# Weight differences issued later, the value product as three matmuls, and block products in runs: one change to a float32 encoder kernel

## The chip, the cores and the metric

The kernel runs on one core of a Trainium2 chip. The metric is the device time of one execution in microseconds (us). Three runs of the kernel before gave 2529.61, 2530.25 and 2532.10 us, so the median is 2530.25 us. A separate execution was profiled, and everything below that speaks of rows, waits or starts is from that one.

## The reference

The reference is a two-layer encoder over 272 tokens (16 meta tokens and 256 others) of width 2048. Each layer has a mixing part (an input projection, attention, a Fourier branch, gates and an output projection) and a feed-forward part. The change touches the feed-forward part alone:

```python
h2 = _rmsnorm(h_stream, norm_ffn[i])
up = h2 @ w_up[i]
u_gate = _dwconv3_centred(up[..., :D_FF], w_conv[i], b_conv[i])
u_val = up[..., D_FF:]
h_stream = h_stream + (jax.nn.silu(u_gate) * u_val) @ w_down[i]
```

`D_FF` is 5632. All of it is float32, and the result of the last layer is wanted for the 256 tokens behind the meta tokens.

## The kernel before

**Chunks.** All large weights come as chunks of 512 KB: 128 partitions by 1024 columns, which is four k-tiles by 256 output channels. `order` lists all chunks of the program in the order of use, group by group. SyncE (SP) loads each into a buffer `raw` (four buffers, L190). ScalarE (ACT) rounds it into `wh` (L230), VectorE (DVE) writes what the rounding lost into `wl` (L233); `wh` and `wl` have three buffers each. `advance` and `pump` write these two operations into the program two chunks (`LOOK = 2`) ahead of the chunk that TensorE (PE) is using. A buffer of `wh` comes free only when PE has used the chunk three places before, so ACT can run at most two chunks ahead.

**A product.** Activations are split in the same way, into a high and a low part. `group` (L272) multiplies one group of chunks: for each k-tile and each of two output tiles it issues three matmuls, `wh` by high (L304), `wh` by low (L305) and `wl` by high (L306). Where high and low parts lie so that one access covers both, and twice the width fits into 512, the first two are one matmul (L300, 512 columns), followed by `wl` by high (L301, 256 columns): this is the fused form. Behind every second of the eight (k-tile, output tile) pairs of a chunk, `group` takes a `step()`, which moves background generators on, and a `pump()`.

**The feed-forward part.** In each layer the 44 tiles of `D_FF` are done in runs (24 and 20 in layer 0; 16, 16 and 12 in layer 1). For each pair of tiles there is a gate group `ug` of four chunks (258 columns in layer 1), whose results pass through DVE and ACT (bias and convolution, L1105 to L1112), and then a value group `uv` of four chunks (256 columns in layer 1, in the fused form, so that ACT copies one half out, L1121, and DVE adds the other, L1122). In layer 0 both groups are unfused and 272 columns wide.

**Block products.** In layer 1 the down projection of the first two runs is not done group by group, but by seven products of sub-blocks (`PRODUCTS`), each over eight pairs of tiles: 56 block chunks for each of the two runs. They stand between the up chunks of the following run: `mixed` (L164 to L173) spreads them. A block chunk takes six matmuls of 512 columns (L1046); here the stationary operand is a combination `cb` of activations, made on ACT and DVE by `combos`, and the moving operand is `wh` or `wl`. When a product's eight blocks are done, DVE adds its result to `C4` (`gather`, L1030). The second run has 64 up chunks and 56 block chunks behind them, the third 48 and 56.

**Weight sums.** Four of the seven products need differences of weight blocks. `weight_sums` makes them earlier, in the feed-forward part of layer 0, as a generator that `step()` moves on (`behindhand`). It makes 16 passes. In a pass it loads four blocks into `b0` to `b3` (one buffer each, DMA issued by ACT at L977, behind a copy of one column at L976 that holds the issue back), takes four differences on DVE (L980, 128x1024), and stores each to memory (DMA issued by ACT at L982, into `ts`). A number given to `yield` is how many steps pass before it goes on: nine steps behind each load it writes the differences that the load completes. A chunk has four steps.

Of the kernel before, what the change touches and what calls it, by code (L numbers as in the profile page):

```python
# [16 lines left out]
P = 128  # L17
D = 2048
# [37 lines left out]
WL_AT.update({(0, k): 16 for k in ("q", "k", "v", "f", "f01", "ga", "gf", "ug", "uv", "d")})  # L56
FR_AT = 12
WL_AT.update({(l, "s"): 40 for l in range(2)})
WL_AT.update({(1, k): 16 for k in ("q", "ga", "gf", "a", "o", "ug")})
BLK = ((0, 16), (16, 144), (144, 272))  # L60

C_COS, C_SIN, C_MASK = 0, T, 2 * T
# [58 lines left out]
def encoder_kernel(ctx, tc, xT, params, consts, bmat, w_in, w_abr, w_four, w_f64, w_out, w_up, w_down, w_blk, outT):  # L121
# [10 lines left out]
    for l in range(DEPTH):  # L132
        def g(w, mg, k0, k1):
            return [(w[l, mg, c], CW) for c in range(k0 // CW, k1 // CW)]
        if l == 0:
            f01 = [g(w_in, IN_F + i, 0, KT) for i in range(2)]
            order.append(((l, "f01"), [ch for pr in zip(*f01) for ch in pr]))
        for i in range(2 if l == 0 else 0, 4):
            order.append(((l, "f", i), g(w_in, IN_F + i, 0, KT)))
        order.append(((l, "k", 0), g(w_in, IN_K, 0, KT)))  # L140
        order.append(((l, "v", 0), g(w_in, IN_V, 0, KT)))
        for i in range(4):
            order.append(((l, "q", i), g(w_in, IN_Q + i, 0, KT)))
        for half in range(2):
            for kind, j in BRANCH_ORDER[half]:
                w, off, n = {"ga": (w_in, IN_GA, KT), "gf": (w_in, IN_GF, KT), "s": (w_four, 0, 8), "a": (w_abr, 0, 8)}[kind]
                order.append(((l, kind, j), g(w, off + j, 0, n)))
            for mg in range(8):
                order.append(((l, "o", half, mg), g(w_out, mg, 8 * half, 8 * half + 8)))
        k0 = 0  # L150
        for c, n in enumerate(FF_SPLIT[l]):
            ups = []
            for i in range(k0 // MG, (k0 + n) // MG):
                ups.append(((l, "ug", i), g(w_up, i, 0, KT)))
                ups.append(((l, "uv", i), g(w_up, FT // MG + i, 0, KT)))
            if l == DEPTH - 1 and c:
                xs_, q0 = [], (k0 - FF_SPLIT[l][c - 1]) // 2
                for p, _ in PRODUCTS:
                    for q in range(FF_SPLIT[l][c - 1] // 2):
                        src = {1: w_blk[2 * (q0 + q), 0], 2: w_blk[2 * (q0 + q) + 1, 0], 3: w_blk[2 * (q0 + q) + 1, 1],  # L160
                               5: tsum[q0 + q][0], 7: tsum[q0 + q][1], 6: tsum[q0 + q][2], 4: tsum[q0 + q][3]}[p]
                        xs_.append((src.rearrange("p (c m) -> p c m", c=CW), (c - 1, p, q)))
                slots = sum(len(chs) for _, chs in ups)
                at = done = 0  # L164
                for u, (key, chs) in enumerate(ups):
                    mixed = []
                    for ch in chs:
                        mixed.append(ch)
                        at += 1
                        while done < len(xs_) and done * slots < at * len(xs_):  # L170
                            mixed.append(xs_[done])
                            done += 1
                    ups[u] = (key, mixed)  # L173
                assert done == len(xs_)
            order += ups
            if l < DEPTH - 1 or c == len(FF_SPLIT[l]) - 1:
                for mg in range(8):
                    order.append(((l, "d", c, mg), g(w_down, mg, k0, k0 + n)))
            k0 += n
# [41 lines left out]
    def split_w(i, a, b, eng=None):  # L221
        if i not in splits:
            h = wp.tile([P, CW, MG * P], F32R, tag="wh", name=f"wh{i}")
            lo = wp.tile([P, CW * MG * P + 64], F32R, tag="wl", name=f"wl{i}")
            o = wl_at[i]
            splits[i] = h, lo[:, o:o + CW * MG * P].rearrange("p (c m) -> p c m", c=CW)
        h, lo = splits[i]
        r = raws[i]
        if eng is None:
            nc.scalar.copy(h[:, a:b], r[:, a:b])  # L230
        else:
            eng.tensor_copy(h[:, a:b], r[:, a:b])
        nc.vector.tensor_tensor(lo[:, a:b], r[:, a:b], h[:, a:b].bitcast(F32), op=ALU.subtract)  # L233
        if b == CW:
            del raws[i]
# [283 lines left out]
    for l in range(DEPTH):  # L519
# [447 lines left out]
        with tc.tile_pool(name=f"ffn{l}", bufs=1) as fp:  # L967
# [2 lines left out]

            def weight_sums():
                tt = nc.vector.tensor_tensor
                for q in range(NPR):
                    b = [fp.tile([P, D // 2], F32, tag=f"b{e}", name=f"b{e}") for e in range(4)]
                    for e, sums in ((0, ()), (1, ((0, 1, 0, 0),)), (3, ((1, 3, 1, 1), (3, 3, 0, 2))), (2, ((2, 2, 3, 3),))):
                        nc.scalar.copy(b[e][:, 0:1], st["cur"][:, 0, 0:1].bitcast(F32))  # L976
                        nc.scalar.dma_start(b[e], w_blk[2 * q + e // 2, e % 2])  # L977
                        yield 9
                        for o, x, y, to in sums:
                            tt(b[o], b[x], b[y], op=ALU.subtract)  # L980
                            yield 2
                            nc.scalar.dma_start(tsum[q][to], b[o])  # L982
                        yield 3

            sets, prods = [], {"have": {}}
            if last:
# [83 lines left out]
            def both(t_, k, at):  # L1070
                a, n = at[0] + lo2, XP + at[1] - at[0]
                if n == XP:
                    return t_[:, k, :, a:a + W2]
                b = 2 * XP * k + a
                s = min(b, 2 * XP * t_.shape[1] - 2 * n)
                return t_.rearrange("p k r n -> p (k r n)")[:, s:s + 2 * n].rearrange("p (r n) -> p r n", r=2)[:, :, b - s:b - s + W2]

            k0 = 0
            for c, n in enumerate(FF_SPLIT[l]):
# [15 lines left out]
                for i in range(k0 // MG, (k0 + n) // MG):  # L1095
                    ps = group((l, "ug", i), xr(lo), W)
                    if i == 0:
                        drain()
                    cs = []
                    for m in range(MG):  # L1100
                        mt = 2 * i + m
                        wc = lambda t: prm[:, P_CW + (l * 3 + t) * FT + mt:P_CW + (l * 3 + t) * FT + mt + 1]
                        bc = prm[:, P_CB + l * FT + mt:P_CB + l * FT + mt + 1]
                        u = fp.tile([P, T], F32, tag="u", name="u", bufs=3)
                        nc.vector.tensor_tensor(u[:, lo:T], ps[m][:, :W], rstdB[:, lo:T], op=ALU.mult)  # L1105
                        cv = fp.tile([P, T], F32, tag="cv", name="cv", bufs=4)
                        nc.scalar.activation(cv[:, lo2:T], u[:, lo2:T], AF.Identity, bias=bc, scale=wc(1))
                        a = max(lo2, 1)
                        nc.vector.scalar_tensor_tensor(cv[:, a:T], u[:, a - 1:T - 1], wc(0), cv[:, a:T], op0=ALU.mult, op1=ALU.add)
                        nc.vector.scalar_tensor_tensor(cv[:, lo2:T - 1], u[:, lo2 + 1:T], wc(2), cv[:, lo2:T - 1], op0=ALU.mult, op1=ALU.add)  # L1110
                        nc.scalar.activation(cv[:, lo2:T], cv[:, lo2:T], AF.Silu)
                        nc.vector.tensor_tensor(cv[:, lo2:T], cv[:, lo2:T], rstdB[:, lo2:T], op=ALU.mult)  # L1112
                        cs.append(cv)
                    ps = group((l, "uv", i), (lambda kt: (both(xHL, kt, X_AT[l]),)) if fused else xr(lo2), W2)
                    for m in range(MG):
                        j = 2 * i + m - k0
                        cv = cs[m]
                        val = ps[m][:, :W2]
                        if fused:
                            v = fp.tile([P, W2], F32, tag="v", name="v", bufs=2)  # L1120
                            nc.scalar.copy(v, ps[m][:, W2:2 * W2])  # L1121
                            nc.vector.tensor_tensor(v, v, val, op=ALU.add)  # L1122
                            val = v
                        if whole:
                            nc.vector.tensor_tensor(sets[c][:, j, :], cv[:, lo2:T], val, op=ALU.mult)
                            continue
                        nc.vector.tensor_tensor(cv[:, lo2:T], cv[:, lo2:T], val, op=ALU.mult)
                        h_ = gH[:, j, lo2 - at_:T - at_]
                        nc.scalar.copy(h_, cv[:, lo2:T])
                        nc.vector.tensor_tensor(gL[:, j, lo2 - at_:T - at_], cv[:, lo2:T], h_.bitcast(F32), op=ALU.subtract)  # L1130
# [79 lines left out]
```

## Time and profile before

| what | value |
|---|---|
| time of the profiled execution | 2528.11 us |
| span of its instructions | 2526.0 us |
| median of three runs | 2530.25 us |
| TensorE busy share | 99% |
| VectorE, ScalarE busy share | 73%, 51% |
| mean granted TensorE clock | 0.999 |
| DMA rate over the span | 221 GB/s |

The profile gives, for every instruction, engine, line, operation, tiles and start. A busy PE is not PE at its peak, because the ends of matmuls are modelled; so what a matmul costs is read below from the distance between starts. "Idle before" names the engine's idle time ahead of an instruction and what ended it. Layer 0's feed-forward part lies between about 522 and 1305 us of the span, the weight sums between 533 and 1197 us, the up and block products of layer 1 between 1804 and 2453 us.

### The profile page before, as it was taken

To read this page: it belongs to the slowest core of one execution; us is meant where nothing else is said; L and a number is where in the kernel's file an instruction comes from. 1 tells how busy PE (TensorE), PEld (TensorE's weight loads), DVE (VectorE), ACT (ScalarE), POOL (GpSimd) and SP (SyncE) were. 2 spreads that over 40 slices of the span, in tenths; PEclk is the share of its full clock that TensorE was granted. 3 is DMA by queue.
4 is the path that set the end of the run, shared out by engine and by line. 5 is a ranking of instruction groups with operands and counts; after the bars stand their busy time and mean duration, and the time that the engine had idled before them with its cause. 6 is when DMAs were issued, how large, how long until landed. Compare 5 with 4: busy or idle time off the path is not lost.

```text
span 2526.0 us, 47879 instructions
## 1 busy us (share of the span) xinstructions
PE 2511.2 (99%) x19404; PEld 2441.2 (97%) x19404; DVE 1852.2 (73%) x2851; ACT 1276.4 (51%) x1857; POOL 18.3 (1%) x37
## 2 busy tenths in 40 slices
PE   9999999999999999999999999999999999999999
PEld 9999999999999999999999999999999989988888
DVE  7687867776776556676556887677766788879985
ACT  6455544554444334444444564445644565556653
POOL 0000000000000000000000000000000000000000
PEclk9999999999999999999999999999999999999999
DMA  7545666568888887787554555666656677778875
GB/s 240 166 157 161 194 185 190 189 225 283 286 282 281 277 292 266 270 288 266 183 179 151 175 157 188 196 201 200 188 189 192 217 243 247 244 249 256 260 244 174
DMA packets 157501, 557.63 MB, mean 221 GB/s; under 512 B 18144, under 2 KB 22112, under 8 KB 157280
## 3 DMA queue, kind: packets, MB, share of 16 engines
q1 hardware_dynamic: 134480, 482.54, 59.5%
q10 hardware_dynamic: 22800, 72.04, 8.1%
q8 instruction: 152, 2.49, 0.4%
q14 instruction: 69, 0.57, 0.1%
HBM read 516.07 MB, written 35.65 MB: 218 GB/s over the span
## 4 chain that ended last, share of the span: by engine, by line
PE 95%; DVE 2%; DMA 1%; ACT 1%; issue 1%; ACTq 0%; SPq 0%; DVEq 0%
PE ps_ug L306 6%; PE ps_ug L304 6%; PE ps_uv L300 6%; PE ps_ug L305 6%; PE ps_x L1046 6%; PE ps_d L306 4%; PE ps_d L304 4%; PE ps_d L305 4%; PE ps_uv L301 3%; PE ps_uv L306 3%; PE ps_uv L304 3%; PE ps_uv L305 3%; PE ps_o L304 2%; PE ps_o L306 2%; PE ps_o L305 2%; PE ps_gf L304 2%
## 5 line engine op out<-in xcount | busy, mean ns | idle before, releaser
L233 DVE TENSOR_TENSOR wl<-raw,wh 128x1024 fp32r<-128x1024 f32 (+1 forms) x883 | 1073.8, 1220 | 442.5 <-ACT wh L230 438.2
L230 ACT CAST wh<-raw 128x1024 fp32r<-128x1024 f32 (+1 forms) x882 | 920.9, 1046 | 853.6 <-PE ps_ug L305 171.4
L306 PE MATMUL ps_ug<-xHL,wl 128*128 128x272 f32 (+1 forms) x1408 | 397.6, 282 | 2.7 <-DVE wl L233 2.7
L304 PE MATMUL ps_ug<-xHL,wh 128*128 128x272 f32 (+1 forms) x1408 | 399.1, 283 | 0.0
L305 PE MATMUL ps_ug<-xHL,wh 128*128 128x272 f32 (+1 forms) x1408 | 397.1, 282 | 0.0
L306 PEld LDWEIGHTS ps_ug<-xHL,wl 128*128 128x128 f32 x1408 | 264.5, 188 | 3.1 <-DVE wl L233 3.1
L305 PEld LDWEIGHTS ps_ug<-xHL,wh 128*128 128x128 f32 x1408 | 264.8, 188 | 2.2
L304 PEld LDWEIGHTS ps_ug<-xHL,wh 128*128 128x128 f32 x1408 | 264.3, 188 | 2.7
L300 PE MATMUL ps_uv<-xHL,wh 128*128 128x512 f32 x704 | 247.7, 392 | 0.0
L306 PE MATMUL ps_d<-gHL,wl 128*128 128x272 f32 (+1 forms) x728 | 208.3, 286 | 2.5 <-DVE wl L233 2.5
L304 PE MATMUL ps_d<-gHL,wh 128*128 128x272 f32 (+1 forms) x728 | 208.8, 287 | 0.0
L305 PE MATMUL ps_d<-gHL,wh 128*128 128x272 f32 (+1 forms) x728 | 207.4, 285 | 0.0
L304 PE MATMUL ps_uv<-xHL,wh 128*128 128x272 f32 x704 | 201.3, 286 | 0.0
L306 PE MATMUL ps_uv<-xHL,wl 128*128 128x272 f32 x704 | 200.7, 285 | 0.0
L305 PE MATMUL ps_uv<-xHL,wh 128*128 128x272 f32 x704 | 199.9, 284 | 0.0
L301 PE MATMUL ps_uv<-xHL,wl 128*128 128x256 f32 x704 | 198.3, 282 | 0.0
L300 PEld LDWEIGHTS ps_uv<-xHL,wh 128*128 128x128 f32 x704 | 132.0, 188 | 28.6
L1046 PE MATMUL ps_x<-wh,cb 128*128 128x512 f32 x448 | 156.6, 393 | 0.0
L304 PE MATMUL ps_ga<-xHL,wh 128*128 128x272 f32 (+1 forms) x512 | 147.0, 287 | 0.0
L304 PE MATMUL ps_gf<-xHL,wh 128*128 128x272 f32 (+1 forms) x512 | 145.8, 285 | 0.1
L304 PE MATMUL ps_o<-mH,wh 128*128 128x272 f32 (+1 forms) x512 | 144.6, 282 | 0.0
L306 PE MATMUL ps_ga<-xHL,wl 128*128 128x272 f32 (+1 forms) x512 | 144.6, 282 | 0.0
(306 smaller groups left out, 5979.8 us busy)
## 6 DMA issues: line engine op xcount, KB each, us to landing
raw<-in_w_up SPq DMA_DIRECT2D x352, 512.0 KB, 4.4
raw<-in_w_in SPq DMA_DIRECT2D x206, 512.0 KB, 3.6
raw<-in_w_down SPq DMA_DIRECT2D x112, 512.0 KB, 4.3
raw<-in_w_out SPq DMA_DIRECT2D x64, 512.0 KB, 3.9
b<-in_w_blk ACTq DMA_DIRECT2D x64, 512.0 KB, 5.0
ts<-b ACTq DMA_DIRECT2D x64, 512.0 KB, 3.6
raw<-ts SPq DMA_DIRECT2D x64, 512.0 KB, 4.5
raw<-in_w_blk SPq DMA_DIRECT2D x48, 512.0 KB, 4.4
```

Of the source, the lines that this page charges most:

```text
L230: nc.scalar.copy(h[:, a:b], r[:, a:b])
L233: nc.vector.tensor_tensor(lo[:, a:b], r[:, a:b], h[:, a:b].bitcast(F32), op=ALU.subtract)
L300: nc.tensor.matmul(o2, h[:, c, sl], ab, start=kt == 0, stop=False)
L301: nc.tensor.matmul(o, lo[:, c, sl], ab[:, 0, :], start=False, stop=kt == nk - 1)
L304: nc.tensor.matmul(o, h[:, c, sl], a, start=kt == 0, stop=False)
L305: nc.tensor.matmul(o, h[:, c, sl], b, start=False, stop=False)
L306: nc.tensor.matmul(o, lo[:, c, sl], a, start=False, stop=kt == nk - 1)
L1046: nc.tensor.matmul(ps[e], cb[:, s_, q - q4], w, start=q == 0 and a == 0, stop=q == n - 1 and a == 2)
```

## The change

Four edits, all in the feed-forward part:

```diff
-WL_AT.update({(1, k): 16 for k in ("q", "ga", "gf", "a", "o", "ug")})
+WL_AT.update({(1, k): 16 for k in ("q", "ga", "gf", "a", "o", "ug", "uv")})
...
-                        while done < len(xs_) and done * slots < at * len(xs_):
+                        while done < len(xs_) and at % 2 == 0 and done * slots < at * len(xs_):
...
             o = wl_at[i]
+            st["new"] = h
...
-                for q in range(NPR):
-                    b = [fp.tile([P, D // 2], F32, tag=f"b{e}", name=f"b{e}") for e in range(4)]
+                b, due = {}, []
+                for q in range(NPR + 1):
                     for e, sums in ((0, ()), (1, ((0, 1, 0, 0),)), (3, ((1, 3, 1, 1), (3, 3, 0, 2))), (2, ((2, 2, 3, 3),))):
-                        nc.scalar.copy(b[e][:, 0:1], st["cur"][:, 0, 0:1].bitcast(F32))
-                        nc.scalar.dma_start(b[e], w_blk[2 * q + e // 2, e % 2])
-                        yield 9
-                        for o, x, y, to in sums:
-                            tt(b[o], b[x], b[y], op=ALU.subtract)
-                            yield 2
-                            nc.scalar.dma_start(tsum[q][to], b[o])
-                        yield 3
+                        if q < NPR:
+                            t_ = fp.tile([P, D // 2], F32, tag=f"b{e}", name=f"b{e}")
+                            nc.scalar.copy(t_[:, 0:1], st["cur"][:, 0, 0:1].bitcast(F32))
+                            nc.scalar.dma_start(t_, w_blk[2 * q + e // 2, e % 2])
+                        yield 5
+                        if due:
+                            one = small.tile([P, 1], F32, tag="one", name="one", bufs=2)
+                            nc.scalar.activation(one, st["new"][:, 0, 0:1].bitcast(F32), AF.Identity, bias=1.0, scale=0.0)
+                        for o, x, y, to in due:
+                            nc.vector.scalar_tensor_tensor(o, x, one, y, op0=ALU.mult, op1=ALU.subtract)
+                            yield 3
+                            nc.scalar.dma_start(to, o)
+                        if q == NPR:
+                            return
+                        b[e] = t_
+                        yield 7 - 3 * min(len(due), 2)
+                        due = [(b[o], b[x], b[y], tsum[q][to]) for o, x, y, to in sums]
...
-                    ps = group((l, "uv", i), (lambda kt: (both(xHL, kt, X_AT[l]),)) if fused else xr(lo2), W2)
+                    ps = group((l, "uv", i), xr(lo2), W2)
...
-                        if fused:
-                            v = fp.tile([P, W2], F32, tag="v", name="v", bufs=2)
-                            nc.scalar.copy(v, ps[m][:, W2:2 * W2])
-                            nc.vector.tensor_tensor(v, v, val, op=ALU.add)
-                            val = v
```

**Weight sums.** A difference is now written behind the next load, not behind its own, and it reads a column `one` that ACT sets to 1.0 from the newest `wh`; so it stands behind that cast. The difference itself is a scalar-tensor-tensor (x times one, minus y) in place of a tensor-tensor. A pass takes 48 steps in place of 56.

In the program, the load of the second block of a pass and the store of the first difference stand as follows on ACT before (second pass; `b_7481` is the block just loaded, `b_7480` the difference that needs it):

```order
L976 COPY b_7481<-wh_7512 128x1
L977 DMA b_7481<-in_w_blk 128x1024
L230 CAST wh_7542<-raw_7388 128x1024
L1111 ACTIVATE cv<-cv 128x272
L230 CAST wh_7572<-raw_7418 128x1024
L982 DMA ts_0_61<-b_7480 128x1024
```

Two casts stand between the load and the store. After the change (first pass; the block is `b_7107`, the difference `b_7006`) the load stands at the first place below, the store at the second:

```order
L979 COPY b_7107<-wh_7017 128x1
L980 DMA b_7107<-in_w_blk 128x1024
L231 CAST wh_7047<-raw_6893 128x1024
...
L1121 ACTIVATE cv<-cv 128x272
L984 ACTIVATE one<-wh_7229 128x1
L979 COPY b_7315<-wh_7229 128x1
L980 DMA b_7315<-in_w_blk 128x1024
L231 CAST wh_7262<-raw_7110 128x1024
L988 DMA ts_0_57<-b_7006 128x1024
```

There are now seven casts between them; the blocks loaded meanwhile are those of the next two differences.

**Block products.** SP loads the chunks in the order in which PE uses them. At the start of layer 1's second run its queue held before (`in_w_up` is an up chunk, `in_w_blk` a block chunk):

```order
L190 DMA raw_23997<-in_w_blk 128x1024
L190 DMA raw_24045<-in_w_up 128x1024
L190 DMA raw_24067<-in_w_blk 128x1024
L190 DMA raw_24089<-in_w_up 128x1024
L190 DMA raw_24111<-in_w_blk 128x1024
L190 DMA raw_24144<-in_w_up 128x1024
```

and now holds:

```order
L190 DMA raw_24323<-in_w_blk 128x1024
L190 DMA raw_24353<-in_w_blk 128x1024
L190 DMA raw_24383<-in_w_up 128x1024
L190 DMA raw_24413<-in_w_up 128x1024
L190 DMA raw_24448<-in_w_blk 128x1024
L190 DMA raw_24484<-in_w_blk 128x1024
```

Counted over the whole of layer 1, 104 runs of block chunks (96 single, 8 of two) become 56 (8 single, 40 of two, 8 of three).

**DVE behind a gate group.** The work that takes a gate group's result stands on DVE between the `wl` of the following chunks. Here is one such place after the change: the first `wl` belongs to the second block chunk behind the group, the last to the first value chunk.

```order
L234 TENSOR_TENSOR wl_26356<-raw_26258,wh_26355 128x1024
L1115 TENSOR_TENSOR u<-ps_ug_0_26226,rstdB 128x258
L1014 TENSOR_TENSOR sx<-g_22328,sx 128x512
L1115 TENSOR_TENSOR u<-ps_ug_1_26227,rstdB 128x258
L1119 SCALAR_TENSOR_TENSOR cv<-u,prm,cv 128x256
L1120 SCALAR_TENSOR_TENSOR cv<-u,prm,cv 128x255
L234 TENSOR_TENSOR wl_26383<-raw_26288,wh_26382 128x1024
```

Before, the same work stood behind the `wl` of the first value chunk (first row) and ahead of the `wl` of the block chunk that follows it (last row):

```order
L233 TENSOR_TENSOR wl_25934<-raw_25836,wh_25933 128x1024
L1105 TENSOR_TENSOR u<-ps_ug_0_25792,rstdB 128x258
L1105 TENSOR_TENSOR u<-ps_ug_1_25793,rstdB 128x258
L1109 SCALAR_TENSOR_TENSOR cv<-u,prm,cv 128x256
L1110 SCALAR_TENSOR_TENSOR cv<-u,prm,cv 128x255
L233 TENSOR_TENSOR wl_25961<-raw_25871,wh_25960 128x1024
```

So that work has moved from between a value and a block chunk to behind two block chunks, in front of the first value chunk's `wl`.

**Value product.** The value group of layer 1 takes three matmuls of 256 columns for each pair, as the gate group does, and the copy and the addition behind it go: 704 matmuls of 512 columns become 1408 of 256. Its `wl` starts 16 columns further into its buffer.

## The prediction

> **What bounds the kernel now.** I read the page first, then who waited for whom, then the timeline where PE waited, then the grouped operations.
>
> ```profile
> span 2526.0 us, 47879 instructions
> PE 2511.2 (99%) x19404; PEld 2441.2 (97%) x19404; DVE 1852.2 (73%) x2851; ACT 1276.4 (51%) x1857; POOL 18.3 (1%) x37
> PE 95%; DVE 2%; DMA 1%; ACT 1%; issue 1%; ACTq 0%; SPq 0%; DVEq 0%
> ```
>
> PE sets the end: 95% of the chain that ended last is PE's. So only two things can move the time: how far apart PE's matmuls start, and the few places where PE waits. The 2% DVE and 1% DMA in the chain are such places. The waits name them:
>
> ```profile
> PE ps_ug L306 <- DVE wl L233: 2.7, 2, 1.7
> PE ps_d L306 <- DVE wl L233: 2.5, 1, 2.5
> DVE b L980 <- DMA b<-in_w_blk: 69.3, 44, 4.9
> ```
>
> PE waits three times for a `wl` in feed-forward layers. DVE stands still for 69.3 us in front of the differences at L980, until a block has landed. Here are the three PE waits, and around the third one the load of the block, the difference and the cast that stands on ACT behind the store. The first row is a stretch without waits:
>
> ```profile
> 700.00:866.00 166.00, 166.00 (x1361) 166.00 (x1360) 112.16 (x137) 73.86 (x102) 0.00 (x0) 1.00 0.83 282
> 1016.50 0.28 PE L305 MATMUL ps_ug<-xHL,wh 128*128 128x272 f32 x1
> 1017.75 0.39 PE L306 MATMUL ps_ug<-xHL,wl 128*128 128x272 f32 x1 [0.96 <-DVE wl L233]
> 1070.55 0.28 PE L305 MATMUL ps_ug<-xHL,wh 128*128 128x272 f32 x1
> 1072.56 0.39 PE L306 MATMUL ps_ug<-xHL,wl 128*128 128x272 f32 x1 [1.73 <-DVE wl L233]
> 1184.03 0.28 PE L305 MATMUL ps_d<-gHL,wh 128*128 128x272 f32 x1
> 1186.77 0.39 PE L306 MATMUL ps_d<-gHL,wl 128*128 128x272 f32 x1 [2.46 <-DVE wl L233]
> 1176.38 0.34 ACTq L977 DMA_DIRECT2D b<-in_w_blk  x1
> 1184.35 1.23 DVE L980 TENSOR_TENSOR b<-b,b 128x1024 f32<-128x1024 f32 x1 [4.86 <-DMA b<-in_w_blk]
> 1186.04 1.04 ACT L230 CAST wh<-raw 128x1024 fp32r<-128x1024 f32 x1 [6.63 <-DVE b L980]
> 1187.00:1188.00 1.00, 1.00 (x8) 1.00 (x8) 1.00 (x2) 0.08 (x1) 0.00 (x0) 0.79 1.02 328
> 1188.00:1191.00 3.00, 3.00 (x15) 3.00 (x14) 2.36 (x5) 1.64 (x4) 0.00 (x0) 0.50 0.91 304
> ```
>
> The load issued at 1176.38 was used at 1184.35, 8 us later; DVE idled 4.86 us, ACT 6.63 us (its store waits for the difference, the cast stands behind the store), and PE's next start came 2.74 us after the last. The last two window rows (PEclk is the third figure from the right) show that the clock was halved right behind it.
>
> **Term 1, the weight sums.** Matmuls of 272 columns start 166.00 / 1361 = 0.122 us apart (first row). The three waits cost 1.25, 2.01 and 2.74 us less 0.12 each: 5.64 us. The clock took 0.21 of the first window and half of 3.00 us in the second: 1.71 us. Together 7.35 us. After the change seven casts stand between a load and its difference, where two stood. A chunk of 24 such matmuls takes 24 x 0.122 = 2.93 us, so the difference comes about 20 us behind the load.
>
> ```profile
> DMA to landing us min/median/max: 2.6/4.6/7.9
> ```
>
> The slowest block landed in 7.9 us, so all three waits go, and the halved clock with the third. The Trainium skill ("TensorE: Matmul & The Clock Gate", HAM oscillation) speaks of idle gaps over about 3.4 us before the clock drops; here 2.46 us idle was enough. By its figure the 1.71 us would not hang on this wait and the term would be 5.64 us; the row decides.
>
> What the edit adds hides under PE. ACT gets 48 columns `one` and DVE 64 longer differences:
>
> ```profile
> L976 ACT COPY b<-wh 128x1 f32<-128x1 f32 x64 | 12.1, 189 | 1.5
> L1109 DVE SCALAR_TENSOR_TENSOR cv<-u,prm,cv 128x256 f32<-128x256 f32 x44 | 21.1, 481 | 0.7 <-ACT cv L1107 0.2
> L1112 DVE TENSOR_TENSOR cv<-cv,rstdB 128x256 f32<-128x256 f32 x44 | 18.5, 419 | 0.2 <-ACT cv L1111 0.2
> ```
>
> A one-column ACT operation takes 189 ns, so 48 take 9 us over some 580 us; the other form costs about 62 ns more, 64 x 0.062 = 4 us of DVE. Behind a waiting difference stand the next `wl`, and on ACT behind a waiting store the next cast. `one` stands directly behind a cast that DVE's preceding `wl` needs too, so it adds no wait. One wait is new: a pass now loads block `b1` two casts (5.9 us) after its store was issued, and the row above has stores among its transfers; a transfer of 7.9 us would hold ACT 2 us. ACT's 6.63 us above cost PE 2.62, so PE had about 4 us in hand, and I take 0, with 2 us as the far end. Shorter passes raise the sums' traffic by 56/48, from 128 transfers of 512 KB in 664 us (101 GB/s) to 118, beside 180 for a chunk in 2.93 us; a load has 20 us to land, so I take 0 for that too.
>
> **Term 2, spacing in layer 1.** Starts of chunks, first in the run without block products, then with them:
>
> ```profile
> 1829.90 0.28 PE L304 MATMUL ps_ug<-xHL,wh 128*128 128x258 f32 x1
> 1835.44 0.28 PE L304 MATMUL ps_ug<-xHL,wh 128*128 128x258 f32 x1
> 1838.22 0.39 PE L300 MATMUL ps_uv<-xHL,wh 128*128 128x512 f32 x1
> 1849.32 0.29 PE L304 MATMUL ps_ug<-xHL,wh 128*128 128x258 f32 x1
> 1852.13 0.28 PE L304 MATMUL ps_ug<-xHL,wh 128*128 128x258 f32 x1
> 2146.66 0.39 PE L1046 MATMUL ps_x<-wh,cb 128*128 128x512 f32 x1
> 2148.06 0.28 PE L304 MATMUL ps_ug<-xHL,wh 128*128 128x258 f32 x1
> 2150.91 0.39 PE L1046 MATMUL ps_x<-wh,cb 128*128 128x512 f32 x1
> 2136.88 0.40 PE L300 MATMUL ps_uv<-xHL,wh 128*128 128x512 f32 x1
> 2139.67 0.40 PE L1046 MATMUL ps_x<-wh,cb 128*128 128x512 f32 x1
> 2243.34 0.39 PE L1046 MATMUL ps_x<-wh,cb 128*128 128x512 f32 x1
> 2246.11 0.28 PE L304 MATMUL ps_ug<-xHL,wh 128*128 128x258 f32 x1
> ```
>
> A gate chunk behind a gate chunk takes 2.77 us (two in 5.54), a fused value chunk 2.775 (four in 11.10). A gate chunk directly behind a fused one takes 2.81, behind a block chunk 2.85 (2148.06 to 2150.91), a fused value chunk behind a block chunk 2.79. A single block chunk takes 1.40, a pair 2.77, so the second 1.37. Unfused work pays for coming behind 512-column work; runs of blocks pay it less often:
>
> - gate chunks behind a block: 47 before, 27 after: 20 x 0.08 = 1.6 us less;
> - block chunks that open a run: 104 before, 56 after: 48 x 0.02 = 1.0 us less;
> - gate chunks directly behind a fused value chunk, 16: 16 x 0.04 = 0.7 us less.
>
> What an unfused value chunk takes, the trace does not show; two rows bound it. The gate chunk (same buffer, same 16-column shift of `wl`, 258 columns) needs 2.77 us; 272 columns need 2.93, so two columns are worth about 0.02, and the low end is 2.75. The high end is the last down group, unfused at exactly 256 columns but from another buffer:
>
> ```profile
> 2514.22 0.28 PE L304 MATMUL ps_d<-gHL,wh 128*128 128x256 f32 x1
> 2522.35 0.28 PE L304 MATMUL ps_d<-gHL,wh 128*128 128x256 f32 x1
> ```
>
> 23 triples in 8.13 us are 0.353 us each, 8 of them 2.83. The gate rows share buffer and shift, so I stay near them: 2.76. In the run without blocks that is 32 x 0.015 = 0.5 us less. With blocks, 28 value chunks stand behind a block (2.76 + 0.08) and 28 do not: 156.8 us against 56 x 2.79 = 156.2, so 0.6 more. Term 2 is -1.6 - 1.0 - 0.7 - 0.5 + 0.6 = -3.2 us; with 2.75 it is -4.1, with 2.83 it is +3.0. The Trainium skill (the same page, Back-to-back issue gap) gives N/2.4 + 2.5 ns a matmul, hence 2.5 ns for the third one and +1.8 us over 704, which would make value chunks slower than the fused ones, not 0.5 us faster; the rows have larger, unequal overheads, and I go by them. Removing 44 copies and 44 additions frees ACT and DVE only.
>
> **Term 3, new waits behind runs.** `wh` has three buffers, so the cast for the chunk behind two blocks can start only when the first block starts, and both `wl` steps have to fit into 2.77 us:
>
> ```profile
> 2244.70 1.22 DVE L233 TENSOR_TENSOR wl<-raw,wh 128x1024 fp32r<-128x1024 f32 x1
> 2246.35 0.28 PE L306 MATMUL ps_ug<-xHL,wl 128*128 128x258 f32 x1
> L1030 DVE TENSOR_TENSOR C<-C,ps_x 128x512 f32<-128x512 f32 x48 | 32.0, 683 | 8.3 <-PE ps_x L1046 8.3
> PEld ps_uv L301 <- DVE wl L233: 0.4, 1, 0.4
> ```
>
> Here, behind one of the eight pairs that exist now, `wl` was ready at 2245.92, 0.43 us before its use. One pair in eight did make PE's weight load wait (the last row, 0.4 us). Afterwards 48 runs have two or three blocks; at the same share, 6 x 0.4 = 2.4 us. The far ends are 0 and, with one further operation of 0.68 us (the L1030 row) in each run's window, as in the last places that the change shows, 48 x (0.68 - 0.43) = 12 us. I take 2.4, since the pairs that exist are the nearest rows.
>
> **Sum.** -7.35 - 3.2 + 2.4 = -8.15 us against the profiled execution's 2528.11 us (span 2526.0 and 2.1 around it): 2520.0. The three runs' median, 2530.25, lies 2.1 above that execution, so I forecast **2522.0 us**.
>
> **Rivals.**
>
> - *Runs starve PE* (slower). DVE cannot make the next `wl` within a run once another operation stands there. For: DVE had 0.43 us to spare, an addition takes 0.68 us, and gate results now come just behind a pair. Against: seven of eight pairs cost nothing, and most runs have no other DVE work. It decides from (7.35 + 3.2 + 5) / 56 = 0.28 us lost in each run; at 0.35 us it is +19.6 - 10.55 = +9 us: 2539.
> - *Unfused value chunks behave like the last down group*: 2.83 us, term 2 is +3.0, sum -1.95: 2528.3, which is no change that counts. For: same width and form. Against: other buffer.
> - *The waits on blocks change place* (the change doesn't do what it says): ACT stands for a store's landing ahead of the next load, and casts come late as before. Term 1 falls to about 0, sum -0.8: 2529.5. For: a slow transfer takes longer than the 5.9 us between. Against: the median is 4.6 us, and PE has about 4 us in hand.
>
> **Chances.** Forecast 0.62 (2517 to 2525), unfused chunks slow 0.14, waits moved 0.12, starved runs 0.12. The low end takes term 2 at -4.1 and term 3 at 0 against the lower of the two bases: 2516.7. The upper end takes in the second and third rival with the spread of the runs: 2531. So 2517 to 2531, leaving out the starved runs. A measurement of this kernel can tell about 0.2%, 5 us, from no change. Faster by more: the forecast and a little of the second, 0.64; within it 0.24; slower 0.12.
>
> **What would show it.** Right: no idle time of DVE for L977's loads, no PE wait on `wl` between 533 and 1200 us, clock 1.00 there; gate chunks behind gate chunks still 2.77 us, value chunks 2.76; single waits of 0.2 us behind runs. Wrong: PE rows of L306 or L1046 waiting for `wl` again and again after 1985 us (first rival), value chunks of 2.8 us or more (second), ACT's casts waiting on its copies ahead of loads (third). Down, output and attention groups should keep their spacing, 0.12 us for 272 columns; if they move, something that I priced at nothing moved them.

## The result: slower, by 0.3%

The changed kernel took 2535.05 us (median of 20 runs, 2533.50 to 2536.81), the kernel before 2526.54 us beside it (20 runs, 2520.53 to 2532.10). The ratio is 1.0031, with an interval of 1.0024 to 1.0038: slower, and above the forecast's range of 2517 to 2531. The head of the page of the kernel after, with its chain's shares:

```profile
span 2533.2 us, 49297 instructions
PE 2524.1 (100%) x20108; PEld 2481.8 (98%) x20108; DVE 1839.5 (73%) x2807; ACT 1267.3 (50%) x1861; POOL 18.3 (1%) x37
PE 97%; DVE 1%; ACT 1%; DMA 0%; issue 0%; ACTq 0%; SPq 0%; DVEq 0%
```

PE has become even more the bound: 97% of the chain, with fewer waits and a longer span. The longest waits of PE in the kernel after (that for the first constants left out), and its stretch of the weight sums:

```profile
PE ps_f L362 <- ACT wh L231: 2.8, 4, 0.8
PE ps_s L341 <- DVE wl L234: 0.9, 2, 0.5
PE ps_pt L854 <- DVE pn L845: 0.6, 1, 0.6
533.00:1200.00 667.00, 667.00 (x5435) 666.92 (x5434) 459.81 (x575) 308.27 (x473) 0.73 (x1) 1.00 0.83 280
```

The rows `ps_ug` and `ps_d` waiting for `wl` are gone, PE is busy all 667 us and the clock is 1.00. So the waits went as forecast. What came in their place is not a wait. The same three windows before and after (the first inside layer 0's output groups, the second inside its down groups, the third inside layer 1's output groups); the count behind PE's busy time is the number of matmuls:

```profile
480.00:520.00 40.00, 40.00 (x330) 40.00 (x329) 32.67 (x56) 24.37 (x42) 0.00 (x0) 1.00 0.55 180
1205.00:1295.00 90.00, 90.00 (x739) 90.00 (x738) 52.24 (x69) 41.69 (x56) 0.00 (x0) 1.00 0.55 178
1766.00:1795.00 29.00, 29.00 (x253) 29.00 (x252) 24.61 (x43) 19.23 (x33) 0.00 (x0) 1.00 0.64 193
```

```profile
480.00:520.00 40.00, 40.00 (x324) 40.00 (x323) 31.23 (x53) 24.03 (x41) 0.00 (x0) 1.00 0.59 176
1205.00:1295.00 90.00, 90.00 (x725) 90.00 (x724) 50.88 (x67) 40.36 (x54) 0.00 (x0) 1.00 0.59 177
1766.00:1795.00 29.00, 29.00 (x244) 29.00 (x244) 23.80 (x41) 17.91 (x30) 0.00 (x0) 1.00 0.60 180
```

In 90 us of down groups PE started 725 matmuls where it had started 739: 124.1 ns in place of 121.8. DVE and ACT did less in these windows, the clock is 1.00 in both, DMA about the same. None of the four edits touches an output group. The groups of the third window by operation, before and then after (busy time, then mean ns of one; the mean has a constant part, so it is the difference that counts):

```profile
L304 PE MATMUL ps_o<-mH,wh 128*128 128x258 f32 x256 | 71.2, 278 | 0.0
L306 PE MATMUL ps_o<-mH,wl 128*128 128x258 f32 x256 | 71.2, 278 | 0.0
L305 PE MATMUL ps_o<-mL,wh 128*128 128x258 f32 x256 | 71.1, 278 | 0.0
```

```profile
L306 PE MATMUL ps_o<-mL,wh 128*128 128x258 f32 x256 | 72.5, 283 | 0.0
L307 PE MATMUL ps_o<-mH,wl 128*128 128x258 f32 x256 | 72.5, 283 | 0.0
L305 PE MATMUL ps_o<-mH,wh 128*128 128x258 f32 x256 | 71.9, 281 | 0.0
```

That is 5 + 5 + 3 ns, 256 times: 3.3 us lost where nothing was edited. The table gives PE's time in each kind of group, as the sum of the distances from each matmul's start to the next one's, in us (output, `ps_o`, and attention, `ps_a`, over both layers). The columns behind "after" are four of the experiments below.

| group | before | after | e1 | e3 | e5 | e7 |
|---|---|---|---|---|---|---|
| layer 0 gate-up | 261.73 | 258.49 | 262.41 | 258.47 | 258.47 | 258.47 |
| layer 0 down | 262.45 | 262.82 | 263.28 | 258.13 | 258.13 | 258.13 |
| output | 182.62 | 187.73 | 187.73 | 182.62 | 182.62 | 182.62 |
| attention | 92.11 | 94.38 | 94.39 | 92.10 | 92.11 | 92.10 |
| layer 1 gate-up | 248.49 | 245.91 | 245.74 | 246.03 | 248.48 | 246.44 |
| layer 1 value | 245.14 | 249.37 | 244.32 | 249.58 | 245.14 | 247.02 |
| block products | 155.22 | 156.78 | 156.35 | 153.98 | 155.23 | 154.75 |
| layer 1 down | 66.32 | 67.26 | 67.27 | 66.32 | 66.32 | 66.31 |
| span | 2526.0 | 2533.2 | 2532.4 | 2518.8 | 2517.5 | 2516.6 |

### The profile page after: what moved, and what is told of

Same layout as the page of the kernel before. It is cut to its first block, busy times and chain, and to the rows that moved or that the text cites. A ratio compares the mean times of both kernels' runs of the same rounds, so it can differ in the third digit from the quotient of the medians.

```text
span 2533.2 us, 49297 instructions
## 1 busy us (share of the span) xinstructions
PE 2524.1 (100%) x20108; PEld 2481.8 (98%) x20108; DVE 1839.5 (73%) x2807; ACT 1267.3 (50%) x1861; POOL 18.3 (1%) x37
## 4 chain that ended last, share of the span: by engine, by line
PE 97%; DVE 1%; ACT 1%; DMA 0%; issue 0%; ACTq 0%; SPq 0%; DVEq 0%
PE ps_uv L305 7%; PE ps_uv L307 7%; PE ps_ug L307 7%; PE ps_uv L306 7%; PE ps_ug L305 7%; PE ps_ug L306 7%; PE ps_x L1056 6%; PE ps_d L305 4%; PE ps_d L307 4%; PE ps_d L306 4%; PE ps_o L306 2%; PE ps_o L307 2%; PE ps_o L305 2%; PE ps_gf L305 2%; PE ps_ga L305 2%; PE ps_ga L307 2%
## 5 line engine op out<-in xcount | busy, mean ns | idle before, releaser
L305 PE MATMUL ps_uv<-xHL,wh 128*128 128x272 f32 (+1 forms) x1408 | 398.9, 283 | 0.0
L306 PE MATMUL ps_uv<-xHL,wh 128*128 128x272 f32 (+1 forms) x1408 | 397.2, 282 | 0.0
L307 PE MATMUL ps_uv<-xHL,wl 128*128 128x272 f32 (+1 forms) x1408 | 396.9, 282 | 0.0
L306 PEld LDWEIGHTS ps_uv<-xHL,wh 128*128 128x128 f32 x1408 | 264.7, 188 | 1.3
L305 PEld LDWEIGHTS ps_uv<-xHL,wh 128*128 128x128 f32 x1408 | 264.3, 188 | 1.2
L307 PEld LDWEIGHTS ps_uv<-xHL,wl 128*128 128x128 f32 x1408 | 264.4, 188 | 0.2
L1056 PE MATMUL ps_x<-wh,cb 128*128 128x512 f32 x448 | 149.8, 395 | 0.0
L306 PE MATMUL ps_o<-mL,wh 128*128 128x272 f32 (+1 forms) x512 | 146.1, 285 | 0.0
L307 PE MATMUL ps_o<-mH,wl 128*128 128x272 f32 (+1 forms) x512 | 145.7, 285 | 0.0
```

Source lines behind the costliest of these rows:

```text
L305: nc.tensor.matmul(o, h[:, c, sl], a, start=kt == 0, stop=False)
L306: nc.tensor.matmul(o, h[:, c, sl], b, start=False, stop=False)
L307: nc.tensor.matmul(o, lo[:, c, sl], a, start=False, stop=kt == nk - 1)
L1056: nc.tensor.matmul(ps[e], cb[:, s_, q - q4], w, start=q == 0 and a == 0, stop=q == n - 1 and a == 2)
```

## The experiments

**What differs in the untouched groups.** The new tile `one` is two buffers of one column in the pool `small`. In the built program each takes 32 bytes of a partition, and every buffer of the pools opened behind `small` has moved up by 64 bytes: `gHL` from byte 133248 to 133312, `mH` from 154432 to 154496, `qH` from 133952 to 134016. The weights' buffers `wh` and `wl` and the feed-forward input `xHL`, which lie ahead, have not. The groups that slowed down are those whose activations come from a moved buffer; layer 0's value groups, which read `xHL`, took 258.4 us before and 258.1 after. Theory A is that the place of these buffers makes the matmuls slower; theory B is that the new order of the work on ACT and DVE does.

**e1: the move alone.** The kernel before, with the tile declared and never used:

```diff
     small = ctx.enter_context(tc.tile_pool(name="small", bufs=4))
+    small.tile([P, 1], F32, tag="one", name="one", bufs=2)
```

> The kernel before with one thing more: 64 bytes are reserved in the pool of small tiles, so every buffer of the mixing and feed-forward parts (gHL, mH, mL, qH, qL, cb, C4) lies 64 bytes further; the weight buffers and xHL stay. Nothing is computed with them. Theory A (place of the moving operand): the output groups of layer 1 go from 115.5 to 120 ns a matmul, those of layer 0 from 122.2 to 124.4, the down groups of layer 0 from 122.2 to 124.4 without their wait, attention groups in the same way; 12 to 16 us slower than before. Theory B (the slower groups of the changed kernel come from its other order or its denser transfers): spacing as before, time within 3 us of before.

Measured: 2534.96 us (2533.20 to 2540.91) beside 2525.83 of before, ratio 1.0040 (1.0024 to 1.0056). Its windows:

```profile
480.00:520.00 40.00, 40.00 (x324) 40.00 (x323) 31.13 (x54) 23.56 (x40) 0.00 (x0) 1.00 0.54 175
1205.00:1295.00 90.00, 90.00 (x725) 90.00 (x725) 51.46 (x68) 40.37 (x54) 0.00 (x0) 1.00 0.56 185
1766.00:1795.00 29.00, 29.00 (x244) 29.00 (x243) 23.40 (x41) 17.44 (x29) 0.00 (x0) 1.00 0.57 185
```

The counts are those of the kernel after: 324, 725, 244. A declaration with no instruction makes the kernel as slow as the whole change does, though by another sum: e1 still has waits on blocks and its value product is fused. Theory A holds, theory B falls. The size was missed: 9.1 us between the medians against the 12 to 16 expected.

One reason stands in the table. Layer 1's gate-up and value groups became 2.75 and 0.8 us shorter, without any regrouping. The gate chunks directly behind a block chunk (47 before and in e1) took 2.791 us in the median where they had taken 2.847. One of them begins at the first start below, and the next block chunk at the second; the prediction shows one of before, 2148.06 to 2150.91:

```profile
2058.97 0.28 PE L304 MATMUL ps_ug<-xHL,wh 128*128 128x258 f32 x1
2061.76 0.40 PE L1047 MATMUL ps_x<-wh,cb 128*128 128x512 f32 x1
```

So the price of coming behind a block hangs on the places of the buffers too: the extra time over a gate chunk behind a gate chunk (2.773 us in both) was 0.074 us before and is 0.018 in e1.

**e2: 128 bytes in place of 64.** The same line with four buffers (`bufs=4`).

> As the last one, with 128 bytes reserved. Theory A does not say which step counts: if places repeat every 128 bytes, output groups of layer 1 are back at 115.5 ns and those of layer 0 at 122.2; if every other place is worse, they stay at 118 or more. Theory B: spacing as before in either kernel.

Measured in one run: 2538.11 us, span 2536.0. Layer 1's output groups stood at 117.8 ns a matmul, layer 0's at 124.4, its down groups at 125.6 (265.17 us / 2112). Not back, and not the same as at 64 bytes either.

**e3: the whole change without the move.** The column is kept in two spare columns of an existing tile:

```diff
-                            one = small.tile([P, 1], F32, tag="one", name="one", bufs=2)
+                            one = mhalf[:, 16 + e % 2:17 + e % 2]
```

> The changed kernel, with the column of ones kept in spare columns of a constant tile, so that no buffer of the mixing part and of layer 0's feed-forward part moves. Theory A: output, attention and down groups have the spacing of before, and the time is 13 to 15 us below the changed kernel's 2535, so 2520 to 2522, below before's median of 2526.5. Theory B: nothing changes, 2534 to 2536.

Measured: 2520.20 us (2518.56 to 2522.03), ratio 0.9976 (0.9967 to 0.9985), span 2518.8. The output, attention and last down groups are back to 0.01 us (table). Against the kernel after, the 64 bytes cost 4.7 us in layer 0's down groups, 5.1 in the output groups, 2.3 in attention, 2.8 in the block products and 0.9 in layer 1's down groups: 15.8, against a difference of spans of 14.4 (small groups went the other way). That is the cost in the changed kernel; in the kernel before it is smaller, because there the shorter gate-up and value groups of e1 stand against it.

**e4: e3 with the value product fused again.** It undoes the third edit, with the tile `v`, so all buffers lie as before:

```diff
-                    ps = group((l, "uv", i), xr(lo2), W2)
+                    ps = group((l, "uv", i), (lambda kt: (both(xHL, kt, X_AT[l]),)) if fused else xr(lo2), W2)
```

> The last one, with the value product of layer 1 fused again (512 and 256 columns, copy and addition back). Theory A with unfused value chunks at 2.827 us against 2.775: 4 us less than the last one, 2516 to 2518. If the freed ACT and DVE work had paid for it: no less than the last one, with PE waits on wl behind runs of blocks.

Measured: 2518.56 us (2517.32 to 2519.85), ratio 0.9970 (0.9959 to 0.9981), span 2516.3. Of the 4 us expected, layer 1's value groups gave 3.5 (246.04 us), but the gate-up groups and block products took 0.7 back, and the span fell by 2.5, the median by 1.6 (the means of the two sets of runs are 2520.03 and 2518.44), a little less than expected. The third edit loses.

**e5: the weight sums alone**, the first edit with its column in place.

```diff
-                            tt(b[o], b[x], b[y], op=ALU.subtract)
...
+                            one = mhalf[:, 16 + e % 2:17 + e % 2]
...
+                            nc.vector.scalar_tensor_tensor(o, x, one, y, op0=ALU.mult, op1=ALU.subtract)
```

> The kernel before with the edit of the weight sums alone, its column kept in mhalf, so that every buffer lies where it lay before. Theory A (the sums remove TensorE's waits in layer 0, and the loss of the changed kernel came from the moved buffers): no wait of TensorE above 0.2 us between 533 and 1200 us, layer 0's gate-up groups 3.3 us shorter in sum and its down groups 2.9, layer 1 as before; profile 2519 to 2522, ratio 0.997 to 0.9985. Rival B (the sums' order on VectorE costs layer 1 something, whatever the places): layer 1's groups 2 us or more longer, ratio 0.999 or above.

Measured: 2519.67 us (2518.53 to 2520.44) beside 2528.54 of before (18 runs, 2523.09 to 2536.45), ratio 0.9970 (0.9959 to 0.9981; the plain quotient of the medians is 0.9965). Its stretch of the weight sums, and what DVE's differences still wait for:

```profile
533.00:1200.00 667.00, 667.00 (x5457) 666.92 (x5457) 463.07 (x578) 309.96 (x476) 0.00 (x0) 1.00 0.82 280
DVE b L986 <- ACT mhalf L984: 3.0, 5, 0.6
```

5457 matmuls in the window where the kernel after has 5435, both without a wait of PE: the 22 are the spacing. DVE waits 3.0 us for the column and no longer for blocks (69.3 before). Layer 1 is as before to 0.01 us in gate-up, value and block products, so rival B falls. Layer 0's down groups fell by 4.3 us where 2.9 were expected: the expectation had left out the half clock behind the wait. The runs' spread fell from 13 us to 2. The waits on `wl` differ between profiled executions (5.2 us in before, 2.0 in e6, 8.6 in e8), so it is likely, though not shown run by run, that the spread went with them.

**e6: the grouping of block products alone.**

```diff
-                        while done < len(xs_) and done * slots < at * len(xs_):
+                        while done < len(xs_) and at % 2 == 0 and done * slots < at * len(xs_):
```

> The kernel before with the grouping of the block products alone; value product fused, sums as before, buffers in place. Theory A: half the entries behind blocks, so layer 1's gate-up groups 2.0 to 2.6 us shorter in sum and its mixing products about 1, layer 0's waits still there; profile 2523 to 2526, ratio 0.998 to 0.9995. Rival C (pairs of blocks starve TensorE of its next operand): waits of 0.3 us or more behind pairs, the groups no shorter, ratio 1.000 or above.

Measured: 2524.13 us (2519.34 to 2530.99), ratio 0.9986 (0.9973 to 0.9999). Layer 1's gate-up groups took 2.12 us less, the block products 0.91 less, the value groups 0.54 more; layer 0's waits were still there, 1.0 us each in `ps_ug` and `ps_d` in this execution, which took 2520.27 us and so less than the 2523 to 2526 expected of it. Theory A holds for the groups. One sign of rival C came, PE's weight loads in `ps_uv` waiting ten times for `wl` (2.8 us in sum, 0.6 at most), but PE's matmuls show no such wait, the gate-up and block groups became shorter, and the ratio lies below 1: rival C falls.

**e7: the value product from the gate's place.** The third edit again, over the gate's 258 columns, which begin two columns (8 bytes) earlier; the two are dropped when the result is read:

```diff
-                    ps = group((l, "uv", i), xr(lo2), W2)
+                    ps = group((l, "uv", i), xr(lo), W)
...
-                        val = ps[m][:, :W2]
+                        val = ps[m][:, lo2 - lo:W]
```

> The changed kernel with its column in mhalf, and the value product as three matmuls over the 258 columns of the gate's moving operand in place of 256 columns that begin two columns later. Theory D (it is the place at which the moving operand begins that makes an unfused value chunk 2.827 us long where a gate chunk takes 2.776): the value chunk falls to 2.76 to 2.78, layer 1's value groups 4 to 5 us shorter in sum than with 256 columns, profile 2514 to 2516, ratio 0.995 to 0.9965. Rival E (it is the value product's own group, its weights or its eviction): the chunk stays at 2.82 or rises by the two columns to 2.85, profile 2518 to 2521.

Measured: 2518.50 us (2517.02 to 2519.28), ratio 0.9967 (0.9954 to 0.9979), span 2516.6. In the run without block products, the starts of the first, second and fourth chunk of a value group and of the gate chunk behind it, in the kernel after and then in e7:

```profile
1841.12 0.28 PE L305 MATMUL ps_uv<-xHL,wh 128*128 128x256 f32 x1
1843.94 0.28 PE L305 MATMUL ps_uv<-xHL,wh 128*128 128x256 f32 x1
1849.60 0.28 PE L305 MATMUL ps_uv<-xHL,wh 128*128 128x256 f32 x1
1852.42 0.28 PE L305 MATMUL ps_ug<-xHL,wh 128*128 128x258 f32 x1
```

```profile
1829.01 0.28 PE L305 MATMUL ps_uv<-xHL,wh 128*128 128x258 f32 x1
1831.79 0.28 PE L305 MATMUL ps_uv<-xHL,wh 128*128 128x258 f32 x1
1837.33 0.28 PE L305 MATMUL ps_uv<-xHL,wh 128*128 128x258 f32 x1
1840.11 0.28 PE L305 MATMUL ps_ug<-xHL,wh 128*128 128x258 f32 x1
```

Four chunks take 11.30 us with 256 columns (2.825 each; the median of such chunks is 2.831 here and 2.827 in e3) and 11.10 with 258 (2.775): more columns in less time. Rival E's chunk of 2.82 to 2.85 falls, theory D's is right. But e7 changed start and width together, so that it is the start and not the width of 256 is not shown: the one other unfused group of 256 columns, the last down group, stood at 116.9 to 120.0 ns a matmul over all the distances tried below, and never at the gate's 115.5. Theory D's gain did not come: the value groups fell by 2.6 us, not 4 to 5, and the time, 2518.50 us, is in rival E's range, not in 2514 to 2516. Directly behind a block a value chunk took 2.836 us in the median, as the gate's do, against 2.827 in e3; block chunks behind a value chunk took 1.393, against 1.373; and one wait for `wl` came, 0.5 us.

**e8: everything moved by 64 bytes**, the weights too:

```diff
     per = ctx.enter_context(tc.tile_pool(name="per", bufs=1))
...
+    per.tile([P, 16], F32, name="pad")
```

> The kernel before with 64 unused bytes a partition ahead of the first buffer of its first pool, so that weights, moving operands and all else are moved by 64 bytes together. Theory F (what counts is how the moving operand's place stands to that of the weights, which the small column had changed): layer 1's output groups stay at 115.6 ns a matmul, layer 0's at 122.2, profile 2526 to 2530. Rival G (the place of the moving operand by itself counts): 120 and 124.4 ns as with the moved column, profile 2532 to 2536.

Measured in one run: 2532.42 us, span 2530.3. Its windows:

```profile
480.00:520.00 40.00, 40.00 (x330) 40.00 (x329) 32.50 (x55) 24.17 (x42) 0.00 (x0) 1.00 0.57 183
1205.00:1295.00 90.00, 89.84 (x735) 89.84 (x735) 52.63 (x69) 41.74 (x56) 0.00 (x0) 1.00 0.60 192
1766.00:1795.00 29.00, 29.00 (x254) 29.00 (x253) 24.27 (x42) 18.30 (x31) 0.00 (x0) 1.00 0.60 194
PE ps_ug L306 <- DVE wl L233: 4.7, 3, 2.5
PE ps_uv L306 <- DVE wl L233: 2.3, 2, 2.0
PE ps_d L306 <- DVE wl L233: 1.6, 1, 1.6
```

The first and third window are those of before to one matmul; in the second, one of the waits on `wl` fell. Layer 1's groups are as before to a few hundredths. The span and the time lie above theory F's range, and the time within rival G's: layer 0's three feed-forward groups, in which the waits on blocks fall, took 4.6 us more than in the profiled execution of before (+4.3, +2.7 and -2.4; the rows show 8.6 us of waits on `wl`, before 5.2; a stretch of 3.41 us at half clock follows a wait in both), and no other group moved by more than about 1. The spacing is what the two theories differ in, and rival G falls: it is the distance between what was moved and what was not, here activations and weights, that counts.

**e9 to e12: other distances.** The kernel of e5, which has no waits on blocks, with unused columns in `small`, 32 bytes each: one, six, eight and sixteen.

```diff
+    small.tile([P, 1], F32, tag="one", name="one", bufs=1)
```

> The kernel with the weight sums in place (no waits of TensorE in layer 0), and 32 unused bytes a partition in small, half of the changed kernel's shift. Theory H (the matmul's spacing follows the moving operand's place against the weights in a pattern that repeats every 256 bytes): layer 1's output groups between 115.6 ns, their place before, and 120.0 ns, their place 64 bytes on; profile 2517 to 2526. Rival I (a step at 64 bytes: the place counts only in whole 64-byte pieces): 115.6 ns, 122.2 for layer 0's output and down groups, profile 2516 to 2519.

> The same with 192 unused bytes. Theory H: neither before's spacing nor that of 64 bytes in all groups; layer 1's output groups between 115.6 and 120 ns, profile 2518 to 2527. Rival J (the move by 64 or by 192 bytes is the same thing, the pattern repeats every 128 bytes, and only the end of a group differed at 128): 120.0 ns, 124.4 for layer 0's output groups, profile 2523 to 2526.

> The same with 256 unused bytes. Theory H: every group's spacing as without the pad, 115.6 ns for layer 1's output groups, 122.2 for layer 0's output and down groups, 229 to 231 for the block products, profile 2516 to 2519. Rival K (no such period; before's place was a lucky one): output groups of layer 1 at 117 ns or more, profile 2521 or more.

> The same with 512 unused bytes. Theory H: as with 256 bytes, 115.6 and 122.2 ns, profile 2516 to 2519. Rival K: 117 ns or more for layer 1's output groups, profile 2521 or more.

Measured, in one run each, with the spacing in ns a matmul (columns: e5, e9, e1, e2, e10, e11, e12; e1 and e2 are kernels of before, with waits on blocks in their spans and feed-forward groups; without them, in the kernel after, layer 0's down groups stood at 124.4 ns at 64 bytes):

| moved by (bytes) | 0 | 32 | 64 | 128 | 192 | 256 | 512 |
|---|---|---|---|---|---|---|---|
| layer 0 output | 122.2 | 125.0 | 124.4 | 124.4 | 124.4 | 122.2 | 122.2 |
| layer 0 down | 122.2 | 126.7 | 124.7 | 125.6 | 126.7 | 122.2 | 122.2 |
| layer 1 output | 115.6 | 117.8 | 120.0 | 117.8 | 120.0 | 115.6 | 115.6 |
| block products | 231.0 | 232.1 | 232.7 | 230.3 | 231.6 | 231.0 | 231.0 |
| span (us) | 2517.5 | 2531.7 | 2532.4 | 2536.0 | 2533.4 | 2517.5 | 2517.5 |

The windows of e9 and of e11:

```profile
1205.00:1295.00 90.00, 90.00 (x712) 90.00 (x712) 49.59 (x65) 39.17 (x54) 0.00 (x0) 1.00 0.52 172
1766.00:1795.00 29.00, 29.00 (x249) 29.00 (x248) 23.64 (x42) 18.29 (x31) 0.00 (x0) 1.00 0.59 187
```

```profile
1205.00:1295.00 90.00, 90.00 (x738) 90.00 (x738) 51.87 (x67) 40.49 (x55) 0.00 (x0) 1.00 0.54 181
1766.00:1795.00 29.00, 29.00 (x253) 29.00 (x252) 25.05 (x42) 17.93 (x30) 0.00 (x0) 1.00 0.59 195
```

At 256 and 512 bytes every group of the table is back and the span is that of e5 to 0.1 us: theory H's repeat holds for these two moves, rival K falls, and so does rival I, since 32 bytes already cost 14 us. Theory H's spans for 32 and 192 bytes were too low (2531.7 and 2533.4 against at most 2526 and 2527): the down groups stood at 126.7 ns, worse than at 64 bytes. With 192 bytes the output groups have rival J's numbers; its repeat of 128 bytes falls by the down groups, 124.7 at 64 and 126.7 at 192, and by e2. The times (2533.65, 2535.81, 2519.41 and 2519.44 us) say the same. One rival more is settled by these runs: that it is ACT's and DVE's buffers, which were moved too, whose place matters. Layer 0's gate-up groups, whose matmuls read only unmoved buffers while ACT and DVE work in moved ones, took 258.5 us in e5, e9 and e10 alike.

**Which is best.** e4, e5 and e7 all beat both kernels, at ratios of 0.9967 to 0.9970 to before; their intervals do not tell them apart.

## Why the prediction was wrong

**The step that failed** is "What the edit adds hides under PE", with its 48 columns `one` priced as ACT time only. Their time does hide; their place does not. The column `one` moved the activations by 64 bytes against the weights, a cost that the prediction put at nothing without a reason. The prediction's last part named the sign ("if they move, something that I priced at nothing moved them"), and those are the groups that moved. The missing term is +14.4 us (after less e3). The kernel before held a hint: it sets the columns at which activations begin (`X_AT`, `Q_AT`, `G_AT`), shifts `wl` (`WL_AT`), and declares a tile `even` of 64 bytes that nothing uses.

Without this term the forecast for the profiled execution, 2520.0, met e3's 2520.73, but in part by luck: the value groups were mis-sized by 4.3 us, and the 2.4 us of term 3 stood against it. Terms 2 and 3 together were forecast at -0.8 us; layer 1's gate-up, value and block groups changed by +0.7 in e3, waits included. The terms one by one:

- **Term 1, -7.35: right.** e5 gave -3.26 in layer 0's gate-up and -4.32 in its down groups, -7.6 together. DVE's longer differences took 1278 ns in place of 1224 (62 ns more were forecast, 54 came), and `one` 199 ns. The rival that waits change place falls. The prediction's reading of the half clock is borne out by two more executions: PE's wait of 2.0 us in e1 and one of 2.5 us in e8 were each followed within 1.3 us by 3.41 us at a clock of 0.50 (the row of e1 is below), while waits of 1.7 us in before and of 2.0 us in e8 were not. The runs' spread is a part of this term that I had not read: before's median of three runs, 2530.25, was 3.7 us above that of the 20 runs, so my 2.1 us from the profiled execution to the median stood on three draws from a spread of 12.

```profile
L986 DVE SCALAR_TENSOR_TENSOR b<-b,one,b 128x1024 f32<-128x1024 f32 x64 | 81.8, 1278 | 3.1 <-ACT one L984 3.0
L984 ACT ACTIVATE one<-wh 128x1 f32<-128x1 f32 x48 | 9.6, 199 | 1.0
747.39:750.80 3.41, 3.41 (x17) 3.41 (x17) 1.43 (x2) 1.23 (x2) 0.00 (x0) 0.50 0.90 350
```

- **Term 2, runs: right where no buffer moves.** Forecast -1.6 - 0.7 in the gate-up and -1.0 in the block products; e3 gave -2.46 and -1.24, e6 (value still fused) -2.12 and -0.91. In the changed kernel it can't be credited: with the move alone, in e1, the gate-up groups took 245.74 us, and with the runs on top, in the kernel after, 245.91.
- **Term 2, the unfused value chunk: wrong, at the far bound.** Forecast 2.76 us, measured 2.827 (median in e3), which is the second rival's 2.83. The value groups came out 4.4 us longer in e3, against +0.1 forecast. I had taken the gate chunk as nearest because it shares buffer and shift; it does not share the start, since a gate chunk's moving operand begins 8 bytes earlier, and not quite the width. e7, with both taken from the gate chunk, has its 2.775; which of the two decides stays open. The Trainium skill ("TensorE: Matmul & The Clock Gate", Back-to-back issue gap) would have made the value chunks slower than fused ones, by an estimate of 1.8 us in all from its formula for a single matmul on its own; that sign was right, with e3 less e4 at 3.5.
- **Term 3, +2.4: too much.** What the chunks directly behind a run took beyond their medians sums to 1.5 us in the kernel after (27 gate chunks with a mean of 2.824 and a median of 2.788, 28 value chunks with 2.843 and 2.825), and to 0.7 to 1.6 us in e3, e4 and e7. The rival of starved runs falls.

The kernel became slower by none of the three rivals. Rival 2 alone would have left it at 2528.3, which is still 7 us faster than what came.

## What to carry to other kernels

Where PE is the bound and a matmul is repeated twenty thousand times, an allocation is an edit: before crediting or blaming a change, look at which buffers it moves against the weights, and compare the spacing of groups that the change does not touch. Here a small new tile cost nothing in spare columns of an existing tile (e3), or where the move came to 256 bytes (e11); placing it behind the buffers that matmuls read should do the same, but was not tried. Then test other starts and widths of an operand: beginning 8 bytes earlier with two columns more was faster here. A bound from a "similar" matmul is only good if its operands have the same distance and width, too.

## What the hardware showed that I had not expected

Matmuls of the rounded float32 parts, each with its own weight load, started 115.6 to 120.0 ns apart at 258 columns and 122.2 to 126.7 ns at 272, with the same instructions and a granted clock of 1.00, as the distance in bytes, within a partition, between the weights and the activations changed. Moves by 256 and 512 bytes gave the spacing of no move (e11, e12), and moving both together by 64 bytes left it as it was (e8). For the block products, where the stationary operand moved and the moving one stayed, it was 230.3 to 232.7 (e1, e2, e9 to e12).

What a gate chunk pays for coming behind a block chunk is not paid at its first matmul: in before the distances (medians of 47 chunks) are 119 to 127 ns for most of the first fourteen of its 24 matmuls and then fall to about 116; in e1, 64 bytes on, they are down to 116 after five.

The Trainium skill ("SBUF — State Buffer", SBUF: two separate sides) says that PE never waits on anyone in reading SBUF; by that a moved buffer costs nothing, and e1 with its 9 us speaks against it, if the cause lies there. Which part of the reading or loading is held up was not measured, so the mechanism stays open; so does why 32 bytes are worse than 64 for the down groups and better for layer 1's output groups.
